# The PEER value products with v standing: 117 of 128 tiles turned, sums brought back by identity products

## The chip, the cores and the metric

One core of a Trainium2 chip runs the whole program: TensorE (PE, with its weight loads PEld), VectorE (DVE), ScalarE (ACT), GpSimd (POOL), and SyncE (SP), which only starts DMAs here. The metric is the device time of one launch in microseconds (us).

## The reference

A decoder trunk of two layers over 256 tokens of 1024 features, float32. Each layer is an attention part (multi-head latent attention in layer 0, native sparse attention in layer 1) and a PEER feed-forward part, each followed by a layer norm of `ALPHA * x + f(x)`. PEER picks for each token, for each of 8 heads, 16 of 16384 experts, and adds up their rows of `v`:

```python
q = (xc @ w_q).reshape(PEER_CHUNK, PEER_HEADS, 2, PEER_DK // 2)
sc = jnp.einsum("thpd,hpnd->thpn", q, subkeys)
...
g = jax.nn.softmax(best, axis=-1)
a = jax.nn.gelu(jnp.einsum("thkd,td->thk", u[experts], xc), approximate=False)
return jnp.einsum("thk,thkd->td", (g * a), v[experts])
```

## The kernel before, in words

The kernel doesn't gather the experts of most tokens. It forms for 192 of the 256 tokens (`ND = 192`) a matrix of weights over all 16384 experts, and multiplies densely with the tables; the other 64 tokens (`GT`) go by gathered rows, which POOL fetches (L565) and DVE multiplies and adds (`g_mac`, L602). A layer's PEER part has two long loops of 128 tiles. The u loop multiplies tiles of `u` with the tokens (eight plain f32 matmuls of 160 columns a tile). The v loop, which the change touches, multiplies the weights W of tile j (128 experts x 192 tokens) with tile j of `v` (128 experts x 1024 features).

The v products are made in the type fp32r from split values: `hi` is `v` cast on ACT (L179), `lo` the rest, subtracted on DVE (L193). W is split too, by `w_hi` (ACT, L900) and `w_lo` (DVE, L905), into a tile of 384 columns: the hi of tokens 0 to 191 first, then the lo of tokens 128 to 191, then the lo of tokens 0 to 127. `mm(out, a, b)` at L273 is a matmul in which `a` stands (128 x 128, loaded as weights) and `b` moves. Before, W stands and `v` moves: `v_mm(j, 0, ...)` makes for tokens 0 to 127 the three products hi·hi, lo-of-v and lo-of-W, over two blocks of 512 features, six matmuls; `v_mm(j, 1, ...)` makes for tokens 128 to 191 four, with hi and lo of W side by side in one standing operand, so that rows 0 to 63 and 64 to 127 of the result are added later (`sum_1`). Sums stay in four PSUM banks, `accs[tt][f]`, from tile 0 to the end. For the last `NT = 10` tiles only the first half is done in the loop; the second half is kept back (`keep` tiles) to run beside the layer norm of tokens 0 to 127.

The order is the program's own; no scheduler moves it. In turn j of the loop stand: the casts and subtractions for the tiles ahead (`hi` to j+3, `lo` to j+2), `w_lo(j + 2)`, `w_hi(j + 3)`, perhaps a `g_mac`, then the matmuls of tile j. `hi` has a ring of four tiles, `lo` of five. SP streams `v` into eight raw tiles. PSUM has eight banks: two each of the tags `acc0` and `acc1`, and four of the tag `mm` (`self.ps()`), which the u loop uses for pairs of tiles until `u_act` (gelu on ACT, L882) and `u_mul` (product on DVE, L891) have read them. The pool `r8` has two tiles of 8 KB a partition, which hold in turn `xF`, `hot`, W of the first 79 tiles, `hN`, and `gb`, the layer norm's gain and bias; POOL loads `gb` in turn 123 of the program (`load_gb`), and DVE needs it first at L351.

Of the kernel before, what the change touches and what calls it, by code (L numbers as in the profile page):

```python
# [19 lines left out]
OP = mybir.AluOpType  # L20
# [4 lines left out]
P = 128  # L25
S = 256
D = 1024
KC = D // P
# [8 lines left out]
ND = S - GT  # L37
# [10 lines left out]
class Kern:  # L48
# [471 lines left out]
    def peer(self, l):  # L520
        tc, nc, I = self.tc, self.nc, self.I
        self.v0 = self.v0s.pop(0)
        self.vlim = self.v0 - 1
        with ExitStack() as es:
# [10 lines left out]
            def slot(j):  # L535
                return slots(j, 1)[:, 0, :]
# [60 lines left out]
            def g_mac(c):  # L597
                t = grow.pop(("v", c))
                if c == 0:
                    nc.vector.tensor_scalar(gacc, t, ggate[:, 0:1], None, op0=OP.mult)  # L600
                else:
                    nc.vector.scalar_tensor_tensor(gacc, t, ggate[:, c:c + 1], gacc, op0=OP.mult, op1=OP.add)  # L602
                g_row()
# [241 lines left out]
            for n in range(4, 17):  # L845
                cur = []
                if n < 16:
                    hi, lo = self.nxt()
                    ps = self.ps()
                    self.proj_T(ps[:, 0:S], hi, lo, xhi, xlo, KC)  # L850
                    cur.append(q_take(n, ps))
                for m in range(2 * n - 8, min(2 * n - 6, 4)):
                    ps = self.ps()
# [37 lines left out]
                    nc.vector.tensor_tensor(y, y, ps, op=OP.mult)  # L891

            WW = {}
            W, late = [], []
            NT = 10

            def w_hi(j):
                if j < P:
                    WW[j] = late[0].tile([P, 3 * P], F32R, tag="w", name="W", bufs=10) if late else W[0][:, j % 5, :]
                    nc.scalar.copy(WW[j][:, 0:ND], slot(j))  # L900

            def w_lo(j):
                if j < P:
                    for o, c in ((2 * P, slice(0, P)), (ND, slice(P, ND))):
                        nc.vector.tensor_tensor(WW[j][:, o:o + c.stop - c.start], slot(j)[:, c],  # L905
                                                WW[j][:, c].bitcast(F32), op=OP.subtract)

            def w_start():
                W.append(self.pr8.tile([P, 5, 3 * P], F32R, tag="r8", name="W"))
                for j in range(3):  # L910
                    w_hi(j)
                w_lo(0)
                w_lo(1)

            dc, dj = 0, None
            self.slow, self.held = True, 0
            self.spread()
            for j in range(P):
                if j == 5:
                    g_x()  # L920
                g_flush(2)
                u_step(j)
                if j == LATE:
                    self.gather()
                if j >= LATE + 6 and j % 2 == 0:
                    self.vlim += 2
                self.slow = j < P - 7
                if j % 2:
                    u_mul()
                elif j:  # L930
                    u_act(j - 2)
                run_side(GB if len(A) > 1 else 2.1 if dj is None or j < dj else 1.15)
                if dj is None and gnext[0]:
                    dj = j + 2
                if not (first or second) and len(A) == 1:
                    es_r.close()

                    hot = self.pr8.tile([P, 2, 4, 2, P, 2], F16, tag="r8", name="hot")
                    A.append((pool(es_1, "slots1").tile([P, P - FIRST, ND], F32, name="A1"), 0, P - FIRST))
                    second.append(g_gen(hot))  # L940
                while dj and dc < len(order) and j >= dj + int((P - 6 - dj) / len(order) * dc):
                    g_dot(dc)
                    dc += 1
                    if dc == len(order):
                        g_weights()
                if done["g"] == ND and j >= P - 5 and not W:
                    w_start()
# [5 lines left out]
            if not W:  # L953
                w_start()


            self.vlim = 1 << 20
            accs = [[self.acc(tt) for _ in range(2)] for tt in range(2)]
            hN = gb = None

            kept = {}

            def v_mm(j, tt, blocks, start=False, stop=False):
                hi, lo, w = kept[j]
                xh, xl, xm = w[:, 0:P], w[:, 2 * P:3 * P], w[:, P:2 * P]
                items = ((xm, hi), (xm, lo)) if tt else ((xh, hi), (xh, lo), (xl, hi))
                for a, (xx, ww) in enumerate(items):
                    go, end = start and a == 0, stop and a == len(items) - 1
                    for f in blocks:
                        self.mm(accs[tt][f], xx, ww[:, f * 512:(f + 1) * 512], go, end)  # L970

            rate, gc = (P - 8 - LEAD) / 64, 0
            gu, late_sums = slice(P - GT, P), deque()
# [18 lines left out]
            for j in range(P):  # L992
                if j == P - FIRST:

                    es_1.close()
                    late.append(es.enter_context(tc.tile_pool(name="late", bufs=10, reuse_waits="tile")))

                    for q in range(P - NT, P - 3):
                        at = (gat, "row", RING) if q < P - 8 else (late[0], "keep", 10)
                        self.alt[self.si + q - j] = lambda at=at: [  # L1000
                            at[0].tile([P, D], F32R, tag=at[1], name="keep", bufs=at[2]) for _ in range(2)]
                hi, lo = self.nxt(j < P - 2)
                w_lo(j + 2)
                w_hi(j + 3)
                if j == 11:
                    hN = self.reload_h()
                if j + 4 == P - 1:
                    gb = self.load_gb(2 * l + 1)
                kept[j] = (hi, lo, WW.pop(j))
                if late_sums:  # L1010
                    late_sums.popleft()()
                while gc < 64 and j >= LEAD + int(rate * gc):
                    g_mac(gc)
                    gc += 1
                    if gc in (60, 64):
                        late_sums.append((g_alpha, g_copy)[gc == 64])
                v_mm(j, 0, (0, 1), j == 0, j == P - 1)
                if j < P - NT:
                    v_mm(j, 1, (0, 1), j == 0)
                    kept.pop(j)  # L1020
            self.new_hT()
            self.warm(AF.Sqrt)
            early = l == 0 and "nsa" in self.parts
# [10 lines left out]
            for j in range(P - 3, P):  # L1034
                v_mm(j, 1, (0, 1))
            lo0 = []
            for f in range(2):
                for j in range(P - NT, P - 3):
                    v_mm(j, 1, (f,), False, j == P - 4)
# [768 lines left out]
```

## Time and profile before

| | us |
|---|---|
| median of 3 runs | 1602.55 (1600.55 to 1604.14) |
| profiled execution | 1603.88 |
| its span | 1601.9 |
| PE busy in the span | 1557.4 |
| first v matmul of layer 0, of layer 1 | 479.27, 1300.68 |
| first matmul of tile 118 in layer 0, in layer 1 | 747.72, 1569.18 |

A page of the profile shows one execution. Rows of the timeline read: start in us, length in us, engine, line, operation, tiles written and read, shapes, how many in a row. Matmuls are pipelined: the length of one (390 ns for 512 columns) is longer than the distance to the next, so distances between starts are what counts. A plain f32 matmul leaves two records, one of fp32r leaves one.

### The profile page before, as it was taken

How to read it: one execution, taken by the hardware profiler on the slowest of the kernel's cores; microseconds unless marked ns; L12 is line 12 of the kernel's file. 1: busy time of each engine (PE TensorE's matmuls, PEld its weight loads, DVE VectorE, ACT ScalarE, POOL GpSimd, SP SyncE). 2: the span in 40 equal slices, each digit the busy share in tenths (PEclk: the TensorE clock that was granted, in tenths of full speed). 3: DMA queues.
4: the chain of work that ended last, by engine and by line, in shares of the span. 5: the costliest groups of instructions: out<-in, count | busy, mean ns of one | idle time of the engine just before them, and what ended most of it. 6: DMA issues, size and time to landing. Idle time of an engine off the chain costs nothing.

```text
span 1601.9 us, 27548 instructions
## 1 busy us (share of the span) xinstructions
PE 1557.4 (97%) x10018; PEld 1396.3 (87%) x10018; DVE 1396.6 (87%) x3245; ACT 683.6 (43%) x1355; POOL 536.3 (33%) x442
## 2 busy tenths in 40 slices
PE   8999999999999999999997999999999999999997
PEld 6879999999998888888785689999999988888886
DVE  5778898999959999999768779799999959999998
ACT  6555201121225555556456753111221245555553
POOL 2010134434326434340442210234443337543420
PEclk9999999999999999999999999999999999999999
DMA  7627899999999999997573257999999999999992
GB/s 242 198 91 229 347 409 408 408 408 351 389 386 363 370 363 345 360 359 286 187 246 101 79 178 248 403 409 408 409 407 345 375 371 397 377 358 344 359 355 91
DMA packets 140519, 510.76 MB, mean 319 GB/s; under 512 B 14144, under 2 KB 17248, under 8 KB 139296
## 3 DMA queue, kind: packets, MB, share of 16 engines
q1 hardware_dynamic: 90416, 325.75, 55.1%
q0 software_dynamic: 49968, 183.26, 30.1%
q8 instruction: 79, 1.29, 0.3%
q14 instruction: 56, 0.46, 0.1%
HBM read 503.19 MB, written 5.24 MB: 317 GB/s over the span
## 4 chain that ended last, share of the span: by engine, by line
PE 78%; DVE 10%; DMA 8%; ACT 2%; issue 1%; POOL 0%; SPq 0%; ACTq 0%; DVEq 0%; POOLq 0%
PE acc L273 45%; PE mm L273 32%; DMA row<-p_ur,xidx 6%; DVE row L578 3%; PE mm L300 1%; DMA nat<-p_u 1%; DMA raw<-a_wv 1%; DVE hot L759 1%; DVE hot L770 1%; DMA xT<-xT 1%; DVE lo L193 0%; DVE idx L641 0%; DVE bnst L347 0%; ACT hi L179 0%; ACT p L1689 0%
## 5 line engine op out<-in xcount | busy, mean ns | idle before, releaser
L273 PE MATMUL acc<-hi,W 128*128 128x512 f32 x1452 | 409.1, 390 | 0.0
L565 POOL DMA_INDIRECT row<-p_v,gidx x128 | 245.1, 1915 | 305.3 <-DVE gacc L602 238.1
L273 PE MATMUL mm<-xF,nat 128*128 128x160 f32 x2304 | 323.0, 300 | 1.9 <-DMA nat<-p_u 1.9
L273 PEld LDWEIGHTS acc<-hi,W 128*128 128x128 f32 x1452 | 272.5, 188 | 57.5
L273 PEld LDWEIGHTS mm<-xF,nat 128*128 128x128 f32 x2304 | 314.6, 190 | 3.1 <-issue 2.5
L273 PE MATMUL acc<-lo,W 128*128 128x512 f32 x968 | 298.8, 390 | 0.0
L193 DVE TENSOR_TENSOR lo<-raw,hi 128x1024 fp32r<-128x1024 f32 (+1 forms) x203 | 247.3, 1225 | 43.7 <-ACT hi L179 37.1
L179 ACT CAST hi<-raw 128x1024 fp32r<-128x1024 f32 (+1 forms) x207 | 215.1, 1045 | 158.8 <-PE acc L273 115.7
L565 POOL DMA_INDIRECT row<-p_ur,gidx x128 | 139.0, 1086 | 280.0 <-DVE row L578 190.1
L273 PEld LDWEIGHTS acc<-lo,W 128*128 128x128 f32 x968 | 181.7, 188 | 38.5
L179 ACT CAST hi<-spare 128x1024 fp32r<-128x1024 f32 x122 | 128.2, 1051 | 109.0 <-PE acc L273 104.3
L602 DVE SCALAR_TENSOR_TENSOR gacc<-row,ggate,gacc 128x1024 f32<-128x1024 f32 x126 | 161.0, 1278 | 0.0
L193 DVE TENSOR_TENSOR lo<-spare,hi 128x1024 fp32r<-128x1024 f32 x122 | 148.8, 1219 | 10.5 <-ACT hi L179 10.5
L578 DVE SCALAR_TENSOR_TENSOR row<-row,gacc 128x1024 f32<-128x1024 f32 x128 | 155.5, 1217 | 0.0
L273 PE MATMUL mm<-xF,more 128*128 128x160 f32 x896 | 125.7, 299 | 0.0
L273 PE MATMUL mm<-xF,raw 128*128 128x160 f32 x896 | 125.5, 300 | 0.0
L273 PEld LDWEIGHTS mm<-xF,more 128*128 128x128 f32 x896 | 122.6, 190 | 0.0
L273 PEld LDWEIGHTS mm<-xF,raw 128*128 128x128 f32 x896 | 122.5, 190 | 0.0
L795 ACT ACTIVATE A<-acc 128x208 f32<-128x208 f32 (+19 forms) x116 | 37.5, 346 | 194.9 <-DVE A L793 168.2
L885 ACT ACTIVATE A<-mm 128x320 f32<-128x320 f32 (+13 forms) x104 | 38.2, 369 | 173.1 <-PE mm L273 171.4
L905 DVE TENSOR_TENSOR W<-A,W 128x128 fp32r<-128x128 f32 (+1 forms) x512 | 107.1, 250 | 0.0
L565 POOL DMA_INDIRECT row<-p_ur,xidx x64 | 65.9, 1030 | 96.2 <-DVE row L578 43.3
(289 smaller groups left out, 2078.7 us busy)
## 6 DMA issues: line engine op xcount, KB each, us to landing
nat<-p_u SPq DMA_DIRECT2D x144, 512.0 KB, 8.6
spare<-p_v SPq DMA_DIRECT2D x64, 1024.0 KB, 8.8
raw<-p_v SPq DMA_DIRECT2D x63, 1024.0 KB, 8.9
raw<-p_u SPq DMA_DIRECT2D x56, 512.0 KB, 14.3
more<-p_u SPq DMA_DIRECT2D x56, 512.0 KB, 16.2
raw<-p_wq SPq DMA_DIRECT2D x32, 512.0 KB, 4.3
raw<-b_wo SPq DMA_DIRECT2D x12, 512.0 KB, 3.6
raw<-a_wo SPq DMA_DIRECT2D x8, 512.0 KB, 4.1
```

Source lines behind the costliest of these rows:

```text
L179: self.nc.scalar.copy(self.his[i], self.raws[i])
L193: e.tensor_tensor(self.los[i], raw, self.his[i].bitcast(F32), op=OP.subtract)
L273: self.nc.tensor.matmul(out, a, b, start=start, stop=stop)
L300: self.nc.tensor.transpose(out, in_, self.ident[:n, :n])
L565: nc.gpsimd.indirect_dma_start(out=t, out_offset=None, in_=table, in_offset=bass.IndirectOffsetOnAxis(ap=at, axis=0))
L578: nc.vector.scalar_tensor_tensor(t, t, 1.0, x, op0=OP.mult, op1=OP.mult, accum_out=d[:, c:c + 1])
L602: nc.vector.scalar_tensor_tensor(gacc, t, ggate[:, c:c + 1], gacc, op0=OP.mult, op1=OP.add)
L759: tt(h[:, 0:2].rearrange("p w g i s -> p (w g) i s"), self.iota4[:, 0, None].to_broadcast([P, 4, P, 2]), selI[:, t0 // 4].rearrange("p w ( ...
L770: tt(o, oj, x[:, :, None, :].to_broadcast(b4), op=OP.mult)
L795: nc.scalar.activation(x[:, m:n, t0:t0 + 4], pv[:, j0 + m:j0 + n], AF.Copy, scale=sc_)
L885: nc.scalar.activation(y[:, :, n:NU], ps[:, :, n:NU], AF.Gelu)
L905: nc.vector.tensor_tensor(WW[j][:, o:o + c.stop - c.start], slot(j)[:, c], WW[j][:, c].bitcast(F32), op=OP.subtract)
```

## The change

For the tiles 0 to 116 (`NV = 117`) the operands change places. A block of 128 features of `hi` stands, and all 384 columns of W move over it; the same block of `lo` stands, and the 192 hi columns of W move. A tile has eight blocks, so sixteen matmuls. The result is turned, features by tokens, and each block has a PSUM bank of its own, `tb[b]`: four of the `acc` tags, four of the tag `mm`. The columns 0 to 191 of a bank hold W's hi on `hi` and on `lo`, the columns 192 to 383 W's lo on `hi`. For these tiles `w_lo` writes the lo of all 192 tokens in one subtraction, in the natural order.

In turn 117 `v_back(b)` copies the second half of a bank to SBUF (ACT) and adds the first (DVE), into a tile `back` of the pool `r8`: four banks in turn 117, two each in turns 118 and 119. The four `acc` banks are then taken anew as `accs` for the tiles 117 to 127, which are multiplied as before. `v_add(b)` turns a block back and adds it to `accs` by two plain f32 matmuls with the identity, for tokens 0 to 127 and 128 to 191; two blocks each in turns 118 to 121.

```diff
-                    for o, c in ((2 * P, slice(0, P)), (ND, slice(P, ND))):
+                    turned = ((ND, slice(0, ND)),)
+                    for o, c in turned if j < NV else ((2 * P, slice(0, P)), (ND, slice(P, ND))):
...
+                turn.append(self.r8("back").rearrange("p a d -> p (a d)"))
...
-            accs = [[self.acc(tt) for _ in range(2)] for tt in range(2)]
+            tb = [self.acc(tt) for tt in (0, 0, 1, 1)] + [self.ps() for _ in range(4)]
...
+            def v_turned(j):
+                hi, lo, w = kept.pop(j)
+                for b in range(KC):
+                    c = slice(b * P, b * P + P)
+                    both = [(tb[b][:, 0:2 * ND], hi, w), (tb[b][:, 0:ND], lo, w[:, 0:ND])]
+                    end = j == NV - 1
+                    for i, (ps, x, m) in enumerate(both[::-1] if end else both):
+                        self.mm(ps, x[:, c], m, j == 0 and i == 0, end and i == 1)
+
+            def v_back(b):
+                x = turn[0][:, b * ND:b * ND + ND]
+                nc.scalar.copy(x, tb[b][:, ND:2 * ND])
+                nc.vector.tensor_tensor(x, tb[b][:, 0:ND], x, op=OP.add)
+
+            def v_add(b):
+                for tt, n in ((0, P), (1, ND - P)):
+                    x = turn[0][:, b * ND + tt * P:b * ND + tt * P + n]
+                    self.mm(accs[tt][b // 4][0:n, b % 4 * P:b % 4 * P + P], x, self.ident, False, False)
...
-                v_mm(j, 0, (0, 1), j == 0, j == P - 1)
-                if j < P - NT:
-                    v_mm(j, 1, (0, 1), j == 0)
+                if j < NV:
+                    v_turned(j)
+                    continue
+                n = j - NV
+                for b in range(4) if n == 0 else range(2 * n + 2, min(2 * n + 4, KC)):
+                    v_back(b)
+                if n == 0:
+                    accs = [[self.acc(tt) for _ in range(2)] for tt in range(2)]
+                v_mm(j, 0, (0, 1), n == 0, j == P - 1)
+                if n == 0:
+                    v_mm(j, 1, (0, 1), True)
                     kept.pop(j)
+                for b in range(2 * n - 2, 2 * n) if 0 < n < 5 else ():
+                    v_add(b)
```

PE at the start of the v loop of layer 0, with the engines whose semaphores an instruction waits for. Before, a tile is ten matmuls into `acc`:

```order
L273 MATMUL mm<-xF,nat 128x160 x7
L273 MATMUL acc<-hi,W 128x512 [waits Activation_49]
L273 MATMUL acc<-hi,W 128x512
L273 MATMUL acc<-lo,W 128x512 [waits DVE_49]
L273 MATMUL acc<-lo,W 128x512
L273 MATMUL acc<-hi,W 128x512 x4
L273 MATMUL acc<-lo,W 128x512 x2
```

After, wide and narrow matmuls alternate, and the blocks 6 and 7 go into `mm` banks that DVE must have read:

```order
L273 MATMUL acc<-W,hi 128x384
L273 MATMUL acc<-W,lo 128x192
L273 MATMUL mm<-W,hi 128x384 [waits PE_49]
L273 MATMUL mm<-W,lo 128x192
L273 MATMUL mm<-W,hi 128x384 [waits PE_49]
L273 MATMUL mm<-W,lo 128x192
L273 MATMUL mm<-W,hi 128x384 [waits DVE_49]
L273 MATMUL mm<-W,lo 128x192
L273 MATMUL mm<-W,hi 128x384 [waits DVE_49]
L273 MATMUL mm<-W,lo 128x192
```

The first tile of the loop now touches all eight banks, where it touched four. PE at the seam, from the last block of tile 116 on, after the change:

```order
L273 MATMUL mm<-W,lo 128x192
L273 MATMUL mm<-W,hi 128x384
L273 MATMUL acc<-hi,W 128x512 [waits DVE_49] x2
L273 MATMUL acc<-lo,W 128x512 x2
L273 MATMUL acc<-hi,W 128x512 x2
L273 MATMUL acc<-hi,W 128x512 [waits DVE_49] x2
L273 MATMUL acc<-lo,W 128x512 x2
L273 MATMUL acc<-keep,W 128x512 x6
L273 MATMUL acc<-ident,back 128x128
L273 MATMUL acc<-ident,back 64x128
L273 MATMUL acc<-ident,back 128x128
L273 MATMUL acc<-ident,back 64x128
```

Tile 117 now waits for DVE, and four identity products follow each of the tiles 118 to 121. DVE at the same place, in the turns 117 to 119, after the change:

```order
L907 TENSOR_TENSOR W<-A_1338,W 128x64
L989 TENSOR_TENSOR back<-acc,back 128x192 [waits Activation_49] x4
L193 TENSOR_TENSOR keep<-raw,keep 128x1024 [waits DMAHW4_49]
L907 TENSOR_TENSOR W<-A_1338,W 128x128
L907 TENSOR_TENSOR W<-A_1338,W 128x64
L602 SCALAR_TENSOR_TENSOR gacc<-row,ggate,gacc 128x1024 [waits DMASW4_49,DVE_49]
L989 TENSOR_TENSOR back<-mm,back 128x192 [waits Activation_49] x2
L193 TENSOR_TENSOR keep<-raw,keep 128x1024
L907 TENSOR_TENSOR W<-A_1338,W 128x128
L907 TENSOR_TENSOR W<-A_1338,W 128x64
L989 TENSOR_TENSOR back<-mm,back 128x192 [waits Activation_49] x2
```

Eight additions have come in between DVE's subtractions for the tiles ahead; the rest stands as it stood.

More of the change, by code (lines that the diff above doesn't have):

```diff
@@ L893, in peer @@
             WW = {}
-            W, late = [], []
+            W, late, turn = [], [], []
             NT = 10
+            NV = P - NT - 1
             def w_hi(j):
```

## The prediction

> **What bounds the kernel now.** I read the page's first lines, then the stretches of the two v loops, then the groups by form, then short stretches of the timeline of TensorE (PE) and of its weight loads (PEld).
>
> ```profile
> PE 1557.4 (97%) x10018; PEld 1396.3 (87%) x10018; DVE 1396.6 (87%) x3245; ACT 683.6 (43%) x1355; POOL 536.3 (33%) x442
> ...
> PE acc L273 45%; PE mm L273 32%; DMA row<-p_ur,xidx 6%; DVE row L578 3%; PE mm L300 1%; DMA nat<-p_u 1%; DMA raw<-a_wv 1%; DVE hot L759 1%; DVE hot L770 1%; DMA xT<-xT 1%; DVE lo L193 0%; DVE idx L641 0%; DVE bnst L347 0%; ACT hi L179 0%; ACT p L1689 0%
> ```
>
> The chain that ended last is 45% matmuls into `acc`, the v products that the change rewrites. The stretches below run from the first v matmul of a layer to the first of tile 118, so 118 tiles of ten matmuls.
>
> ```profile
> core 0: us, PE busy (x) PEld busy (x) DVE busy (x) ACT busy (x) POOL busy (x), PEclk, DMA share, GB/s
> 479.27:747.72 268.45, 268.45 (x1182) 221.68 (x1182) 255.68 (x423) 156.61 (x242) 110.76 (x61) 1.00 0.96 356
> 1300.68:1569.18 268.50, 268.50 (x1182) 221.60 (x1182) 256.71 (x425) 158.09 (x244) 123.56 (x61) 1.00 0.97 361
> ```
>
> PE has no gap, DVE is busy for 95% and the DMA engines for 96%. So PE sets the pace, but the other two have only 4 to 5% to give. A tile takes 268.45/118 = 2.275 us, a 512-column matmul 227.5 ns. Is that a price per column or a fee per matmul? The projections have 256-column matmuls of the same type:
>
> ```profile
> 809.83 1.07 PE L273 MATMUL mm<-hT,hi 128*128 128x256 f32 x8
> 810.74 1.07 PE L273 MATMUL mm<-hT,lo 128*128 128x256 f32 x8
> ```
>
> Eight in 0.91 us, 114 ns each: exactly half. So streaming costs 0.444 ns a column and there is no fixed fee, as long as the next weight load is hidden. The change lowers the columns of a tile from 10 x 512 = 5120 to 8 x (384 + 192) = 4608, and raises its weight loads from 10 to 16. What a load costs beside a short matmul decides.
>
> **The loads.** Groups by form, of PEld (mean ns of one in the second field behind the bar):
>
> ```profile
> L273 PEld LDWEIGHTS acc<-hi,W 128*128 128x128 f32 x1452 | 272.5, 188 | 57.5
> L273 PEld LDWEIGHTS <-hot 128*128 128x128 f16 x640 | 40.2, 97 | 7.7 <-issue 5.0 <-DVE hot L759 0.6 <-DVE hot L764 0.3
> L273 PEld LDWEIGHTS mm<-pT,vN 128*64 128x64 f32 x192 | 12.8, 137 | 6.4 <-issue 1.2 <-ACT pT L1221 0.5 <-ACT p L1243 0.2
> ```
>
> A four-byte load of 128 columns is recorded with 188 ns, one of 64 columns with 137: 0.8 ns a column, some 100 ns for 128, on a fixed latency that pipelines. A two-byte load (97) is far cheaper. Here is a four-byte load behind a short matmul, in two places of the timeline:
>
> ```profile
> 70.71 0.22 PE L273 MATMUL mm<-cmask,identb 128*128 128x128 bf16 x1
> 70.74 0.48 PE L273 MATMUL acc<-hi,oT 128*128 128x512 f32 x1
> ...
> 285.85 0.39 PE L273 MATMUL acc<-hot 128*128 128x128 f16 x4
> 286.08 0.35 PE L273 MATMUL mm<-xF,nat 128*128 128x160 f32 x1
> ...
> 70.71 0.30 PEld L273 LDWEIGHTS acc<-hi,oT 128*128 128x128 f32 x2
> ...
> L273 PE MATMUL acc<-hi,W 128*128 128x512 f32 x1452 | 409.1, 390 | 0.0
> ```
>
> 128 two-byte columns stream in (286.08 - 285.85)/4 = 57 ns. Behind such a matmul the matmul of type fp32r with four-byte weights (`hi,oT`) is stamped 0.03 us later and lasts 0.48 instead of 0.39: it waited 0.09 more, so the step was 0.11 to 0.12 us, not 0.057. Its load began with the matmul ahead (both at 70.71), not earlier. A second witness are matmuls with only 64 moving columns:
>
> ```profile
> 846.24 1.89 PE L273 MATMUL mm<-kcp,qu 128*128 128x64 f32 x16
> 145.21 0.60 PE L273 MATMUL mm<-subT,qT 128*128 128x128 f32 x4
> ...
> L273 PE MATMUL mm<-subT,qT 128*128 128x128 f32 x128 | 18.3, 276 | 0.1
> ```
>
> Sixteen starts over about 1.89 - 0.28 us, 107 ns each, no faster than passes with twice the columns ((0.60 - 0.28)/3 = 108). So a four-byte load needs 107 to 115 ns from the start of the matmul ahead of it.
>
> **The change, step by step.**
>
> 1. *Turned tiles (117 of each layer).* The pair of a block: the 384-column matmul streams 0.444 x 384 = 170.6 ns and hides the load of `lo`. The 192-column matmul would stream 85 ns, but the next `hi` load, which starts with it, takes 107 to 115. I take 112, between the two witnesses. A tile: 8 x (170.6 + 112) = 2.261 us, against 2.275; over 234 tiles it saves 3.3 us. Ends: 107 ns gives 2.221 and 12.7 us saved, 118 ns (the load as slow as the slower spacings suggest, plus a few ns) gives 2.309 and 7.9 us lost. The Trainium skill, page "TensorE: Matmul & The Clock Gate", section "LDWEIGHTS (loading the stationary operand)", prices a load by its columns at 1.2 GHz, 106.7 ns for 128. By it this term would be 13.3 us saved and the end some 10 us lower than I forecast; the trace's 0.8 ns a column agrees with the slope, and the 0.11 to 0.12 us above speak for a little more.
>
> 2. *Adding the sums back.* Sixteen plain f32 matmuls a layer. The scores `subT,qT` are 64 such matmuls and have 128 records: two passes each, 108 ns a pass. So 32 x 0.109 = 3.5 us a layer (3.7 at 115 ns). They stand between the tiles 118 to 121, where PE has no gap today (42 matmuls without one in the row at 747.72 below), so all of it is on the path: +7.0 us.
>
> 3. *Emptying the banks at the seam (tile 117).* Its first matmuls take the banks that `v_back` 0 and 1 must have read. ACT can copy bank 0 when tile 116 has done its first block, 2 us before its end, and is free by then. DVE stands later:
>
> ```profile
> 742.87 0.35 ACT L900 CAST W<-A 128x192 fp32r<-128x192 f32 x1
> 745.56 0.42 DVE L905 TENSOR_TENSOR W<-A,W 128x128 fp32r<-128x128 f32 x2
> 745.90 1.22 DVE L193 TENSOR_TENSOR keep<-raw,keep 128x1024 fp32r<-128x1024 f32 x1
> ...
> 745.44 0.62 PE L273 MATMUL acc<-hi,W 128*128 128x512 f32 x2
> 747.72 9.70 PE L273 MATMUL acc<-keep,W 128*128 128x512 f32 x42
> ...
> 758.78 1.21 DVE L193 TENSOR_TENSOR lo<-spare,hi 128x1024 fp32r<-128x1024 f32 x1
> 760.48 0.62 PE L273 MATMUL acc<-lo,W 128*128 128x512 f32 x2
> 768.87 0.68 DVE L990 TENSOR_TENSOR hN<-hN,mm 64x512 f32<-64x512 f32 x1
> ```
>
> PE starts tile 117 at 745.44 and DVE reaches the place of `v_back` at 745.9. One add over 192 columns lies between 0.25 (128 columns) and 0.68 us (512), so about 0.32; the copy is like the 0.35 of L900. With one W subtraction a tile less, DVE comes some 0.3 us earlier: PE waits 0.2 to 1.2 us, I take 0.6 a layer, +1.2 us. The eight adds delay DVE's later `lo` tiles by 2.6 us. Today the last `lo` is done at 759.99 and read at 760.48; PE will come 4.1 us later (steps 2 and 3), so that is covered, by 2 us.
>
> 4. *The start of the loop.* Eight banks instead of four: four are the `mm` banks of the last u tiles, free only after gelu and product. In layer 0 the last product is done at 480.58, when PE is at block 5 of 8. In layer 1 it isn't:
>
> ```profile
> 480.09 0.49 DVE L891 TENSOR_TENSOR A<-A,mm 128x320 f32<-128x320 f32 x1 [2.63 <-ACT mm L882]
> ...
> 1300.68 0.73 PE L273 MATMUL acc<-hi,W 128*128 128x512 f32 x2
> ...
> 1301.04 1.05 ACT L179 CAST hi<-raw 128x1024 fp32r<-128x1024 f32 x1 [5.01 <-DMA raw<-p_v]
> 1303.26 0.96 DVE L891 TENSOR_TENSOR A<-A,mm 128x320 f32<-128x320 f32 x2
> ```
>
> ACT was held by a late v tile, and the two last products end at 1303.75 and 1304.22. PE reaches block 6 at 1300.68 + 6 x 0.283 = 1302.4, waits twice, and ends tile 0 at about 1304.6 instead of 1302.95: +1.6 us (0 if the tile comes in time, 1.7 at most).
>
> 5. *One W subtraction instead of two, and other cover.* DVE saves some 0.1 us a tile, worth nothing while PE leads. `hi` is now read until the end of its tile, so ACT's next cast comes 0.3 us later, three tiles ahead of its use: nothing. `gb` lands in the slot that `back` now holds, so its load waits for the last identity product:
>
> ```profile
> 724.23 0.59 POOL L324 DMA_DIRECT2D gb<-ln_g  x1
> 761.36 0.69 DVE L344 SCALAR_TENSOR_TENSOR hN<-hN,acc 128x512 f32<-128x512 f32 x1 [1.03 <-PE acc L273]
> 764.44 0.74 DVE L351 SCALAR_TENSOR_TENSOR hN<-hN,lnw,gb 128x512 f32<-128x512 f32 x1
> ...
> DMA to landing us min/median/max: 5.0/9.8/12.0
> ```
>
> Counted from the end of tile 116 the last product ends at 0.6 + 2.28 + 4 x 1.365 + 3.5 = 11.8 us, its use comes at 11.8 + 6 x 1.365 + 3.1 = 23.1 (3.1 as between the two DVE rows); with two issues of 0.59 and 9.8 it lands at 22.8. Just covered; the slowest landing would cost 2 us in layer 0. POOL has nothing else queued behind it. I count 0, with 2 for the range.
>
> *Sum.* -3.3 + 7.0 + 1.2 + 1.6 = +6.5 us. The profiled execution took 1603.88 us (span 1601.9), 1.3 over the median of the runs, 1602.55. From that median: 1609.
>
> **Rivals.**
>
> *A, the short matmul costs its columns (faster).* If the load of the next `hi` is already taken in ahead of the 192-column matmul, a pair costs 576 x 0.444 = 256 ns, a tile 2.048: 53 us saved, 9.8 paid, 1559. Between this and my price the sign turns where the load costs 108.5 ns (9.8 us saved), and under 107 it is faster by over 0.2%. For it: PEld is idle for 17% of the loop. Against it: the load at 70.71 starts with the matmul ahead, though PEld had room. The Trainium skill states this rule on the same page, section "Back-to-back issue gap": N/2.4 + 2.5 ns a matmul, which here would be 1.96 us a tile and 1538; the same section warns that it leaves the load out at small N, and the 227.5 ns of 512 columns (215.8 by the formula) don't fit it.
>
> *B, a narrow fp32r matmul is slower.* No fp32r matmul under 256 columns is in the trace. At the price of plain f32, two passes of some 0.85 ns a column (136 ns for 160 in the u loop: 12 in 1.63 us), 192 columns would take 326 ns, a tile 3.97: +397 us, 2009. Nothing shows it.
>
> ```profile
> 329.74 1.79 PE L273 MATMUL mm<-xF,nat 128*128 128x160 f32 x12
> 331.37 2.88 PE L273 MATMUL mm<-xF,raw 128*128 128x160 f32 x20
> ```
>
> *C, the seams grow.* DVE comes to `v_back` a whole `lo` and row product late (2.5 us instead of 0.6) in both layers, and `gb` is 2 us late twice: +7.8 on my sum, 1617.
>
> **How the numbers follow.** My forecast 0.78, A 0.12, B 0.04, C 0.06. A measurement of this kernel can tell about 0.2%, 3.2 us, from no change. Within my forecast the load's price moves the sum between -12.7 and +7.9 where I have -3.3: slower in three of four, the same for 107 to 110 ns, faster only at the very end. So slower 0.66, same 0.15, faster 0.19 (0.12 of it A). Range: lowest load price with the small seams, 1602.55 - 12.7 + 7.0 + 0.4 + 0 = 1597; highest, 1602.55 + 7.9 + 7.4 + 2.4 + 1.7 + 2 = 1624. It holds my forecast and C, so 0.84 less its tails.
>
> **What will show it.** Pairs of PE in the loop: from a 384- to a 192-column start about 171 ns, back about 112, and PEld close to full. If the second is 85, A. Rows `acc<-ident,back` with 64 passes in all over 7 us; a short wait of PE on DVE at tile 117; a wait at the first tile of layer 1. DVE's share of the loop falls. Wrong I would be most easily by the load's price: each 5 ns of it are 9.4 us.

## The result, and the profile after

The changed kernel takes 1624.08 us (median of 4 runs, 1621.92 to 1624.99), the kernel before in the same comparison 1601.83 (1600.55 to 1604.14): 1.0135 times as long, interval 1.0118 to 1.0153, so 22 us slower. The profiled execution took 1624.99 us (span 1623.1). The page's busy line, and the head of its chain:

```profile
PE 1576.6 (97%) x11486; PEld 1502.3 (93%) x11486; DVE 1388.4 (86%) x3027; ACT 687.6 (42%) x1371; POOL 505.9 (31%) x442
...
PE mm L273 48%; PE acc L273 27%; DMA row<-p_ur,xidx 4%; DVE row L578 3%; PE mm L300 1%; DVE lo L193 1%; DMA spare<-p_v 1%; DMA raw<-a_wv 1%; DMA nat<-p_u 1%; DVE hot L770 1%; DVE idx L641 1%; DVE gacc L602 1%; DMA xT<-xT 1%; DVE hot L759 0%; ACT hi L179 0%
```

PE still sets the pace, and weight loads are now in flight for 93% of the span instead of 87%. The v loops of both kernels, from the first v matmul of a layer to the start of the last (after the span of each, the busy time of each engine). Before:

```profile
core 0: us, PE busy (x) PEld busy (x) DVE busy (x) ACT busy (x) POOL busy (x), PEclk, DMA share, GB/s
479.27:771.25 291.98, 291.98 (x1290) 241.05 (x1290) 277.68 (x464) 171.08 (x263) 112.11 (x63) 1.00 0.91 337
1300.68:1591.77 291.09, 291.09 (x1282) 240.19 (x1281) 277.77 (x464) 167.59 (x259) 123.56 (x61) 1.00 0.90 336
```

After; the last two rows are only the turned tiles, from the first matmul of tile 0 to the last of tile 116:

```profile
481.24:781.41 300.17, 299.49 (x2024) 292.18 (x2023) 272.73 (x357) 172.93 (x271) 102.49 (x63) 1.00 0.90 329
1312.91:1612.84 299.93, 299.02 (x2015) 291.44 (x2015) 273.29 (x357) 169.23 (x267) 104.72 (x61) 1.00 0.88 326
...
481.24:748.24 267.00, 267.00 (x1875) 266.92 (x1873) 246.34 (x302) 155.82 (x243) 99.99 (x59) 1.00 0.96 354
1312.91:1580.57 267.66, 267.43 (x1874) 266.95 (x1873) 247.84 (x304) 157.08 (x245) 103.58 (x59) 1.00 0.96 355
```

The loops are 8.19 and 8.84 us longer: 17.0 of the 21.1 us between the two profiled executions. The other 4.1 lie outside the loops (2.0 ahead of the first, 2.1 between the two). The turned tiles are hardly the reason: 117 tiles took 268.45 x 117/118 = 266.2 us before, and take 267.0 and 267.7 now. Most of the loss comes after them. The seam, on PE and on DVE:

```profile
748.06 0.36 PE L273 MATMUL mm<-W,hi 128*128 128x384 f32 x1
749.10 0.77 PE L273 MATMUL acc<-hi,W 128*128 128x512 f32 x2 [0.68 <-DVE back L989]
...
751.55 1.53 PE L273 MATMUL acc<-keep,W 128*128 128x512 f32 x6
752.92 1.53 PE L273 MATMUL acc<-ident,back 128*128 128x128 f32 x8
754.38 1.65 PE L273 MATMUL acc<-keep,W 128*128 128x512 f32 x6
755.87 1.52 PE L273 MATMUL acc<-ident,back 128*128 128x128 f32 x8
```

```profile
747.22 1.22 DVE L193 TENSOR_TENSOR keep<-spare,keep 128x1024 fp32r<-128x1024 f32 x1
748.36 0.42 DVE L907 TENSOR_TENSOR W<-A,W 128x128 fp32r<-128x128 f32 x2
748.69 1.15 DVE L989 TENSOR_TENSOR back<-acc,back 128x192 f32<-128x192 f32 x4
```

PE starts its last turned matmul at 748.06 and would start tile 117 some 0.18 us later; it starts at 749.10, so 0.87 us are lost to the adds that DVE begins at 748.69. A group of eight identity passes takes 752.92 to 754.38, 1.46 us. Four groups a layer: 5.84 us.

Inside the turned tiles, the loads (PEld) show what a pair costs:

```profile
600.14 0.19 PEld L273 LDWEIGHTS acc<-W,hi 128*128 128x128 f32 x1
600.25 0.19 PEld L273 LDWEIGHTS acc<-W,lo 128*128 128x128 f32 x1
600.43 0.19 PEld L273 LDWEIGHTS acc<-W,hi 128*128 128x128 f32 x1
600.53 0.19 PEld L273 LDWEIGHTS acc<-W,lo 128*128 128x128 f32 x1
```

The next load follows 0.11 us after the load of a `hi` block, which is the narrow matmul's turn (109 ns in single records), and 0.18 us after that of a `lo` block, the wide one's turn (176 ns). PE's own starts at the same place look otherwise:

```profile
600.14 0.25 PE L273 MATMUL acc<-W,lo 128*128 128x192 f32 x1
600.23 0.36 PE L273 MATMUL acc<-W,hi 128*128 128x384 f32 x1
600.42 0.25 PE L273 MATMUL acc<-W,lo 128*128 128x192 f32 x1
```

From a narrow to a wide start it is 0.09 us, close to the 0.085 that the prediction had set as the sign of rival A. But a pair is 0.28 us long, and not the 0.256 of A. The wide matmul is stamped at 600.23, and the load behind it only starts at 600.25, 0.11 us after the load before it: the stamp seems to come while the wide matmul still waits for its weights. With 96 columns (run 3 below) the starts lie 0.24 and 0.04 us apart, and the pair is as long as here. So the starts of PE don't tell the two prices apart. Read by the loads, the narrow matmul lasts as long as a load, and the wide one longer.

### The profile page after: what moved, and what is told of

It is laid out like the page before. It is cut to its first block, busy times and chain, and to the rows that moved or that the text cites. A ratio compares the mean times of both kernels' runs of the same rounds, so it can differ in the third digit from the quotient of the medians.

```text
span 1623.1 us, 30277 instructions
## 1 busy us (share of the span) xinstructions
PE 1576.6 (97%) x11486; PEld 1502.3 (93%) x11486; DVE 1388.4 (86%) x3027; ACT 687.6 (42%) x1371; POOL 505.9 (31%) x442
## 4 chain that ended last, share of the span: by engine, by line
PE 77%; DVE 12%; DMA 7%; ACT 2%; issue 2%; SPq 0%; POOL 0%; ACTq 0%; DVEq 0%; POOLq 0%
PE mm L273 48%; PE acc L273 27%; DMA row<-p_ur,xidx 4%; DVE row L578 3%; PE mm L300 1%; DVE lo L193 1%; DMA spare<-p_v 1%; DMA raw<-a_wv 1%; DMA nat<-p_u 1%; DVE hot L770 1%; DVE idx L641 1%; DVE gacc L602 1%; DMA xT<-xT 1%; DVE hot L759 0%; ACT hi L179 0%
## 5 line engine op out<-in xcount | busy, mean ns | idle before, releaser
L565 POOL DMA_INDIRECT row<-p_v,gidx x128 | 216.7, 1693 | 336.2 <-DVE gacc L602 269.9
L273 PE MATMUL mm<-W,hi 128*128 128x384 f32 x936 | 284.7, 360 | 0.2 <-DVE A L891 0.2
L273 PE MATMUL acc<-W,hi 128*128 128x384 f32 x936 | 284.5, 360 | 0.0
L273 PE MATMUL acc<-W,lo 128*128 128x192 f32 x936 | 234.2, 250 | 0.0
L273 PE MATMUL mm<-W,lo 128*128 128x192 f32 x936 | 234.2, 250 | 0.0
L273 PEld LDWEIGHTS mm<-W,lo 128*128 128x128 f32 x936 | 178.8, 191 | 0.0
L273 PEld LDWEIGHTS acc<-W,lo 128*128 128x128 f32 x936 | 178.8, 191 | 0.0
L273 PEld LDWEIGHTS mm<-W,hi 128*128 128x128 f32 x936 | 175.8, 188 | 0.6 <-DVE A L891 0.6
L273 PEld LDWEIGHTS acc<-W,hi 128*128 128x128 f32 x936 | 175.8, 188 | 0.0
```

What stands on the lines that cost most here:

```text
L273: self.nc.tensor.matmul(out, a, b, start=start, stop=stop)
L565: nc.gpsimd.indirect_dma_start(out=t, out_offset=None, in_=table, in_offset=bass.IndirectOffsetOnAxis(ap=at, axis=0))
```

## The experiments

Two theories of the turned tiles stood against each other: by the first a short matmul lasts as long as the next four-byte load, by the second it costs its columns, and something else (a bank taken twice, a fee, a wait) makes up the sum. Beside them stood the question of what the seam and the identity products cost. "Pair" is a 384- and a 192-column matmul with their loads; it is read from windows that lie inside the loop, as 120 us over half the matmuls counted. (A window also counts the matmuls in flight at its edges, so these prices come out 0.3 to 0.6% low: between single starts the pair of 284 is 284.5.) The columns are as in the windows above.

**1. The changed kernel again, on another chip.**

> The changed kernel once more, on the chip of the next three. Theory: its cost is in places that repeat: a pair of the loop at 285 ns (109 from a narrow start's weight load, 176 for the wide matmul), identity blocks of 1.46 us four times a layer, a wait of about 1 us at tile 117; about +22 us over before. Rival: some 4 us of the 21 in the first profile lie outside the two v loops (PE's rows stand 2.2 us late before the first v loop and gain 2 more between the loops) and are chance: then this run shows another shift there and +17 to +20 in all.

1619.82 against 1604.44 us, 1.0088 times (1.0067 to 1.0110). Its loops are 300.18 and 299.91 us long, the same as in the first run to 0.03 us; its first v matmul is at 479.24, not 481.24. So the 17 us in the loops come again, and the 2.0 ahead of the first loop don't. The 2.1 between the loops mostly do (531.1 us from loop to loop, 529.4 before, 531.5 in the first run). Still, nothing ties either to the change: over all fourteen profiles of this case the first v matmul stands at 478.3 to 481.9 and the way from loop to loop is 526.2 to 531.5 us long, with 481.9 in a kernel that turns nothing (run 12) and 526.2 in one that does (run 6). The two comparisons, +22 and +15, lie on both sides of 17; the second is below both numbers that were expected.

**2. and 3. The narrow matmul with 256 and with 96 columns.** The first moves 64 columns more than needed; the second leaves out the products with `lo` for tokens 96 to 191.

```diff
-                    both = [(tb[b][:, 0:2 * ND], hi, w), (tb[b][:, 0:ND], lo, w[:, 0:ND])]
+                    both = [(tb[b][:, 0:2 * ND], hi, w), (tb[b][:, 0:2 * P], lo, w[:, 0:2 * P])]
...
+                    both = [(tb[b][:, 0:2 * ND], hi, w), (tb[b][:, 0:ND // 2], lo, w[:, 0:ND // 2])]
```

> The narrow matmul moves 256 columns instead of 192 (the 64 more add lo of v on lo of W for tokens 0 to 63). Load theory: the step from a narrow to the next wide matmul is set by the weight load, 109 ns, and 256 columns stream in 114: +5 ns at most, 0 to +9 us over the changed kernel. Column theory (0.444 ns a column and a fixed fee of 15 ns for each matmul): +28 ns a pair, +53 us.

> The narrow matmul moves 96 columns instead of 192 (leaves out lo of v for the tokens 96 to 191 in the turned tiles). Load theory: no gain, 0 to -3 us against the changed kernel. Column theory with a fee for each matmul: -43 ns a pair, -80 us.

1639.38 us (1.0209, 1.0183 to 1.0236) and 1620.79 (1.0098, 1.0070 to 1.0125), beside 1619.82 for the unchanged copy on the same chip. So 256 columns cost 20 us more than 192, over the 0 to 9 of the load theory and far under the 53 of the columns, and 96 columns gain nothing. One window inside the loop: of the changed kernel and of the one with 256 columns, with a second window in the later tiles, and of the one with 96.

```profile
520.00:640.00 120.00, 120.00 (x846) 120.00 (x845) 110.36 (x136) 68.98 (x106) 46.63 (x28) 1.00 0.97 357
680.00:740.00 60.00, 60.00 (x421) 60.00 (x420) 55.15 (x67) 34.24 (x53) 19.22 (x12) 1.00 0.95 347
```

```profile
520.00:640.00 120.00, 120.00 (x821) 120.00 (x820) 106.74 (x130) 66.69 (x104) 45.41 (x28) 1.00 0.96 350
680.00:740.00 60.00, 60.00 (x402) 60.00 (x401) 52.03 (x64) 32.53 (x52) 21.90 (x13) 1.00 0.94 341
```

```profile
520.00:640.00 120.00, 120.00 (x845) 120.00 (x845) 110.09 (x134) 68.52 (x105) 48.09 (x29) 1.00 0.98 359
```

846 and 845 matmuls: half the columns, the same pair of 284 ns. PE is never idle here, so no other engine covers up a gain: the load is the floor, and columns below it are free. With 256 columns a pair takes 292 ns here and 298 (60 us over 201) in the later tiles, against 284 and 285. The starts of PE and of the loads are equally far apart in this run, and single records put the narrow matmul at 117 to 118 ns in both places, 8 to 9 more than a load, and the wide one at 176 ns here and 182 in the later tiles. So the wide one's price varies too.

**4. Identity products of constant width.** Each pair of identity products stands 128 and 64 columns wide (tokens 0 to 127 and 128 to 191). Here both stand 128 wide, the second padded with zeros.

```diff
-                x = turn[0][:, b * ND:b * ND + ND]
+                x = turn[0][:, b * 2 * P:b * 2 * P + ND]
...
-                    x = turn[0][:, b * ND + tt * P:b * ND + tt * P + n]
-                    self.mm(accs[tt][b // 4][0:n, b % 4 * P:b % 4 * P + P], x, self.ident, False, False)
+                    x = turn[0][:, b * 2 * P + tt * P:b * 2 * P + tt * P + P]
+                    self.mm(accs[tt][b // 4][:, b % 4 * P:b % 4 * P + P], x, self.ident, False, False)
...
+                if n == 0:
+                    nc.gpsimd.memset(turn[0].rearrange("p (b t) -> p b t", b=KC)[:, :, ND:2 * P], 0.0)
```

> The second identity product of a block stands with 128 columns (64 of them zeros) instead of 64. Theory: PE pays about 94 ns each time the width of the standing operand changes between 128 and 64, since the next load then waits for the matmul ahead; without the changes 32 passes a layer take 109 ns, a group of eight 0.87 us instead of 1.46: -2.3 us a layer, -4.7 us in all. Rival: the passes are slow because they wait for the additions on DVE or because each is the only one of its bank: groups stay at 1.46 us, 0 us.

1616.21 us (1.0064, 1.0037 to 1.0090), 3.6 less than the unchanged copy. The timeline of PE:

```profile
755.28 1.05 PE L273 MATMUL acc<-ident,back 128*128 128x128 f32 x8
756.09 1.63 PE L273 MATMUL acc<-keep,W 128*128 128x512 f32 x6
```

More weights to load, yet a group takes 0.81 us (755.28 to 756.09) instead of 1.46. The loop of layer 1 is 297.23 us long instead of 299.91, 2.7 less, which is about 4 x 0.65. In layer 0 this execution had slower pairs (830 matmuls in the same 120 us; 290 ns between single starts, against 284.5 in layer 1), and the loop gained nothing. The times alone would not show the gain: those of this kernel lie at 1610.54 to 1621.16, those of the unchanged copy at 1617.26 to 1622.57. What costs is the change of the standing width. In the changed kernel's single records the eight steps of a group take 0.11, 0.20, 0.16, 0.20, 0.21, 0.20, 0.16 and 0.20 us; the second, fourth, sixth and eighth are those at which the width changes. There the next load starts 0.20 us after the matmul ahead, and not with it, and the steps behind, 0.16 and 0.21, are dearer too. In the run with constant width seven steps take 0.11 and the last 0.03. Spread over the group, a change costs 0.65/4 = 0.16 us.

**5. Without the identity products.** The turned sums are left out of the result.

```diff
                 for b in range(2 * n - 2, 2 * n) if 0 < n < 5 else ():
-                    v_add(b)
+                    pass
```

> Leaves out the identity products, so the sums of the tiles 0 to 116 don't reach the output; all else is as in the changed kernel. Theory: the products are wholly on the path, 5.84 us a layer: -11.7 us against the changed kernel, about +4 over before. Rival: DVE or ACT bounds the tiles 118 to 127 (DVE has the additions of v_back in front of its subtractions), so taking PE's work out only uncovers a wait: -5 us or less.

1609.28 against 1601.68 us: 1.0045 (1.0027 to 1.0063). Loop of layer 0, and PE at the seam:

```profile
480.51:775.08 294.57, 293.81 (x1992) 287.88 (x1992) 272.68 (x357) 172.94 (x271) 102.59 (x63) 1.00 0.91 336
```

```profile
748.35 0.76 PE L273 MATMUL acc<-hi,W 128*128 128x512 f32 x2 [0.67 <-DVE back L989]
750.79 10.19 PE L273 MATMUL acc<-keep,W 128*128 128x512 f32 x42
```

294.57 instead of 300.17: 5.6 us a layer go. The groups had taken 5.84 and the first matmul behind each 0.12 more than its price, 6.3 together; in their place come 0.7 us in which PE waits for DVE's subtractions, 0.25 of them in one step among the 42. So next to nothing hides the identity products. Run 6, which has them and ran on the same chip, takes 12.6 us more. What is left, 2.6 and 3.2 us a layer in the loops, is the seam, the turned tiles and these waits: turning loses even without the identity products.

**6. The narrow matmul a block later.** If two matmuls in a row into one bank cost something, `lo` of block b after `hi` of block b+1 mends it.

```diff
+                if 0 < j < NV - 1:
+                    for b in range(KC + 1):
+                        if b < KC:
+                            self.mm(tb[b][:, 0:2 * ND], hi[:, b * P:b * P + P], w, False, False)
+                        if b > 0:
+                            a = b - 1
+                            self.mm(tb[a][:, 0:ND], lo[:, a * P:a * P + P], w[:, 0:ND], False, False)
+                    return
```

> In the tiles 1 to 115 the matmul on lo of block b comes after that on hi of block b+1, so neighbours write different PSUM banks; the same matmuls and loads otherwise. Theory that the 5 ns a pair above the streaming price come from two matmuls in a row into one bank: a pair falls from 285 to 280 ns, -9 us. Rival (the moving operand or the load beside it costs them): 0, within 3 us of the changed kernel.

1621.85 us, 1.0133 (1.0111 to 1.0155). 845 matmuls in the window where the changed kernel has 846: banks aren't it.

**7. and 8. The kernel before, with each 512-column matmul cut in two:** 256 + 256, and 320 + 192. Nothing is turned, only columns and loads change.

```diff
                     for f in blocks:
-                        self.mm(accs[tt][f], xx, ww[:, f * 512:(f + 1) * 512], go, end)
+                        for o, e in ((0, 256), (256, 512)):
+                            self.mm(accs[tt][f][:, o:e], xx, ww[:, f * 512 + o:f * 512 + e], go and o == 0, end and o > 0)
```

> The kernel before, with each 512-column matmul of the v loop cut into two of 256 columns: twenty matmuls and loads a tile instead of ten, the same columns. Theory that streaming is 0.444 ns a column without a fee and a load needs 109 ns: a half takes 114, a tile 2.275, 0 us. Rival that each matmul with a load of its own carries 4 to 5 ns (as the 256-column matmuls on W with their 118 suggest): a tile 2.36, +20 us over the kernel before.

> The kernel before, with each 512-column matmul of the v loop cut into 320 and 192 columns. Load theory: the 192 columns cost the next load, 109 ns instead of 85, the 320 columns 142 to 147: 251 to 256 ns for what took 227.5, a tile 2.51 to 2.56, +55 to +67 us. Column theory: 2.275 a tile, 0 us, or +20 with a fee of 4 to 5 ns a matmul.

The halves: 1623.85 us (1.0131, 1.0110 to 1.0152). 320 + 192: 1681.18 (1.0501, 1.0478 to 1.0524), 79.5 more. Windows of the halves, then of 320 + 192:

```profile
520.00:640.00 120.00, 120.00 (x1002) 120.00 (x1001) 107.70 (x178) 65.03 (x101) 45.00 (x27) 1.00 0.94 342
680.00:740.00 60.00, 60.00 (x532) 60.00 (x531) 56.98 (x94) 34.70 (x54) 23.41 (x15) 1.00 0.98 363
```

```profile
520.00:640.00 120.00, 120.00 (x930) 120.00 (x929) 99.93 (x164) 60.55 (x94) 41.13 (x26) 1.00 0.90 317
```

Cutting 512 into 320 and 192 raises 227 ns to 120/465 = 258, with the same columns: 109 for the load behind the narrow one and about 149 for 320 columns. The columns theory is dead in a second place. The load theory had the kind of the loss and not its size, 55 to 67 us: it took 142 to 147 for the 320 columns. The halves cost 120 ns each in the first 79 tiles and 113 in the later ones, where W lies in other tiles; at 113 cutting in two is free. That a 256-column step has two prices fitted neither theory.

**9., 11. and 12. Does the place of W set that price?** Number 9 is number 7 with the first tile of W moved by 64 bytes; number 11 is the kernel before with the later tiles of W moved by as much; number 12 is number 9 again, one execution on another chip.

```diff
-                W.append(self.pr8.tile([P, 5, 3 * P], F32R, tag="r8", name="W"))
+                W.append(self.pr8.tile([P, 2 * D], F32R, tag="r8", name="W")[:, 16:16 + 15 * P].rearrange("p (j c) -> p j c", j=5))
...
-                    WW[j] = late[0].tile([P, 3 * P], F32R, tag="w", name="W", bufs=10) if late else W[0][:, j % 5, :]
+                    WW[j] = late[0].tile([P, 3 * P + 32], F32R, tag="w", name="W", bufs=10)[:, 16:16 + 3 * P] if late else W[0][:, j % 5, :]
```

> As the run with 256-column halves, but W's tile of the first 79 tiles starts 64 bytes later in its partition. In that run a step took 120 ns where W (standing) and v (moving) began at the same place within 128 bytes, and 113 where they were 64 bytes apart (W of the later tiles). Theory that this place decides: the first 79 tiles come down to 113 too, 79 x 20 x 6.5 ns x 2 = -20 us, back to the time of the kernel before within 3 us. Rival that it is the other things that change at tile 79 (the pool, the end of the slots of A, less traffic): no change, +20 us over before.

> The kernel before, with W's tiles from tile 79 on starting 64 bytes later, so that W and v begin at the same place within 128 bytes as in the first 79 tiles. There a 512-column step takes 226.7 ns, after tile 79 it takes 228.9. If the place is the cause, 39 tiles x 10 x 2.2 ns x 2 = -1.7 us, the steps at 226.7 throughout; if not, the steps stay and the time too.

> The kernel of the run before last once more. Its executions lay between 1602 and 1626 us, and the profiled one (1625) had 256-column steps of 118 ns in both parts of the loop. Theory that the price of a step is settled anew in each execution, for all of it: another profile shows steps of 113 where the time is near 1602, and 118 where it is near 1625. Rival that the steps stay at 118 and the spread comes from elsewhere (DMA, the u loops): steps of 118 whatever the time.

Number 9: 1614.53 us, 1.0073 (1.0032 to 1.0113), but its six runs spread from 1602.29 to 1625.66. Number 11: 1605.89, 1.0016 (1.0000 to 1.0031), so no gain; its 512-column steps after tile 79 went from 229 ns to 231, and not to the 227 of the first tiles. Number 12: 1606.36 beside 1600.83. Windows of number 9's profiled execution, and of number 12's:

```profile
520.00:640.00 120.00, 120.00 (x1022) 120.00 (x1021) 109.77 (x182) 66.27 (x103) 47.78 (x28) 1.00 0.95 345
680.00:740.00 60.00, 60.00 (x512) 60.00 (x511) 55.36 (x90) 32.79 (x51) 22.41 (x15) 1.00 0.96 346
```

```profile
520.00:640.00 120.00, 120.00 (x1061) 120.00 (x1060) 114.03 (x189) 69.07 (x106) 50.05 (x28) 1.00 0.97 364
680.00:740.00 60.00, 60.00 (x532) 60.00 (x531) 57.48 (x94) 34.16 (x54) 20.96 (x14) 1.00 0.97 363
```

One program, 117 ns a step in the one execution (118 between single starts) and 113 in the other. The later tiles, which number 9 doesn't move, went from 113 to 117. So the place of W doesn't set the price of a 256-column step by itself. Nor is the price settled once for an execution: number 7 has both in one loop, run 4 has 290 ns a pair in layer 0 and 284.5 in layer 1, and the kernel before has both prices in its projections, a few us apart (below). The granted clock was 1.00 in all these stretches. What sets the price stays open.

**10. Only the wide matmuls** (one execution). The narrow ones are left out in tiles 1 to 115, and with them the products with `lo`.

```diff
-                    for i, (ps, x, m) in enumerate(both[::-1] if end else both):
+                    for i, (ps, x, m) in enumerate(both[::-1] if end or j == 0 and False else both if j in (0,) else both[:1]):
```

> Leaves out the narrow matmuls (lo of v) in the tiles 1 to 115: eight 384-column matmuls with their loads a tile. DVE then sets the pace, so only the steps inside a tile count. If streaming is 0.444 ns a column a step is 171 ns; if it is 0.417 ns a column (213 of the 227 ns of 512 columns) and 13 to 16 ns for each matmul, 173 to 176.

1589.75 us; DVE sets the pace then (119.34 of 120 us busy) and PE waits once a tile. Inside a tile PE doesn't wait:

```profile
604.30 0.87 PE L273 MATMUL mm<-W,hi 128*128 128x384 f32 x4
605.00 0.86 PE L273 MATMUL acc<-W,hi 128*128 128x384 f32 x4
605.70 0.86 PE L273 MATMUL mm<-W,hi 128*128 128x384 f32 x4
```

Four in 0.70 us, 175 ns a matmul with no narrow neighbour. So the wide matmul's price in the changed kernel, 284 - 109 = 175, is its own. It is 77% of a 512-column step, not 75%.

## Why the prediction was wrong

The sign of the sum was right, and so were the places: a floor under the narrow matmul, identity products on the path, a wait at the seam. The sign of the turned tiles, a gain, was not. The sum was 6.5 us, against 17.0 in the loops and 15 to 22 in the two comparisons.

| term, us | forecast | in the profiled loops |
|---|---|---|
| turned tiles | -3.3 | +1.6 |
| identity products | +7.0 | +11.7 |
| seam | +1.2 | +1.7 |
| start of the loop of layer 1 | +1.6 | +0.7 |
| not forecast | 0 | +1.3 |
| sum | +6.5 | +17.0 |

The turned tiles are 0.8 + 1.5 us over 266.2, less 0.7 that is the start's wait. What is not forecast is mostly the first matmul behind each identity group: from 752.92 to 755.87 there are 2.95 us, less 1.46 for the group and 6 x 0.2275 for six 512-column matmuls, so 0.12 more, eight times.

*Step 1, the term with the wrong claim.* The load's price was taken as 112 ns and is 109, nearer the lower witness; by itself that would have saved another 5.6 us. The wide matmul was taken as 384 x 0.444 = 170.6 ns, because 256 columns had cost exactly half of 512, "and there is no fixed fee". It costs 175, over 1872 pairs 8 us more, and in the later tiles a little more still. The inference failed, not the row: the 114 ns of the projections is one of two prices that 256 columns have, as runs 7, 9 and 12 show. The other one stood in the trace before as well, 20 us ahead of the row that was read:

```profile
789.59 2.05 PE L273 MATMUL mm<-hT,hi 128*128 128x256 f32 x16
791.47 1.10 PE L273 MATMUL mm<-hT,lo 128*128 128x256 f32 x8
```

Sixteen in 1.88 us are 118 ns each. No one line runs through 113, 175 and 227. One through 120 (run 7) and 227 does better: some 0.42 ns a column and 13 ns a matmul, an estimate from these two, give 147 and 174 for 320 and 384 columns, where about 149 and 175 were measured. So these rows speak for a fixed fee a matmul, with the 113 as the exception. The Trainium skill, page "TensorE: Matmul & The Clock Gate", section "LDWEIGHTS (loading the stationary operand)", has the load at its columns over 1.2, an estimate of 106.7 ns for 128; the 109 here come close. The slope in the Trainium skill's section "Back-to-back issue gap" on the same page, 1/2.4 ns a column, is about that between 384 and 512 columns, (227.5 - 175)/128 = 0.41, but the whole formula gives 162.5 at 384 where 175 were measured.

*Step 2, the costliest miss.* The passes were priced by the attention scores, whose standing operand keeps one width, 0.109 us each. Run 4 shows that price right for constant width (0.81 us a group, 3.2 a layer against the 3.5 forecast). The identity products alternate between 128 and 64 columns, and that makes it 5.84, or 4.7 us more for both layers. That all of it lies on the path was right (run 5). The price of a change could be read before, where the standing width goes from 128 to 64 columns behind three such passes:

```profile
79.75 0.49 PE L300 MATMUL mm<-ident,p 128*128 128x128 f32 x3
80.17 0.87 PE L273 MATMUL mm<-pT,vN 128*64 128x256 f32 x8
```

The three take 0.42 us, and not 3 x 0.109 = 0.33: the last one, ahead of the change, takes 0.20.

*Step 3.* 0.87 us a layer against 0.6, within its bounds; the releaser is the one named, DVE's add. *Step 4* was sized too high. The order of DVE's work at the start of layer 1 was as told, but the products were done earlier. PE's two waits at a bank are in these rows of wide matmuls:

```profile
1314.42 0.36 PE L273 MATMUL mm<-W,hi 128*128 128x384 f32 x1
...
1315.09 0.44 PE L273 MATMUL mm<-W,hi 128*128 128x384 f32 x1 [0.23 <-DVE A L891]
...
1315.57 0.45 PE L273 MATMUL mm<-W,hi 128*128 128x384 f32 x1
...
1315.94 0.36 PE L273 MATMUL acc<-W,hi 128*128 128x384 f32 x1
```

Three pairs take 1.52 us instead of 0.85, so 0.7 are lost.

*Step 5* held: no wait at `gb`, and DVE's share of the turned tiles fell from 95 to 92 or 93%.

*The rivals.* A (columns set the price) fell to runs 3 and 8. B (a narrow fp32r matmul is slower) fell as well: 192 and even 96 columns are no dearer than a load. C (DVE late by a whole turn) didn't come: 0.68 us of recorded wait, not 2.5. The range ended at 1624 and missed by 0.1 us; it let the load's price vary and held the 170.6, and the identity products at 3.5 to 3.7 a layer, as if they were measured, though both were carried over from other shapes. Which side of its end the time fell on was chance: the 17.0 us of the loops alone, or the ratio of run 1, would have lain within.

No version here that makes all the products beats the kernel before. The best of the turned ones, with constant width, is at 1616.21, and 1609.28 without the identity products.

## What to carry to other kernels

Count the weight loads before the columns: with four-byte weights a matmul of 96 or 192 columns costs here the 109 ns of the next load, so a swap of operands that saves a tenth of the columns and makes 16 loads of 10 saves nothing. Take the price of a matmul from a row of its own length, or from two lengths on both sides, and keep it as a range where only one other length is in the trace. Where small matmuls must be put on a full PE, let all of them stand equally wide, even padded with zeros: that took a group from 1.46 to 0.81 us.

## What was not expected of the hardware

- A change of the standing width between 128 and 64 columns costs some 0.16 us (run 4): the step at a change takes 0.20 us and the one behind it 0.16 or 0.21, where steps of constant width take 0.11.
- A 256-column fp32r matmul with its own load costs 113 ns in one execution (run 12) and 118 in another of the same program (run 9), in long stretches without a wait, and both prices also stand in one execution (113 and 120 in run 7). The two profiled times go the same way, 1606 and 1625 us; run 9 spread from 1602 to 1626. It was not found what sets the price.
- A four-byte load of 128 columns is 109 ns from the start of the matmul ahead, whether that moves 96 or 192 columns.
